# Seven products for eight in two FFN down products of each layer

## The chip, the cores and the metric

The kernel runs on one core of a Trainium2 chip. The metric is the device time of one execution in microseconds (us). A comparison takes the median of several runs. Everything below is float32 in and out.

## The reference, cut to what matters

A two-layer trunk on 256 tokens of width 2048. Each layer has a token mixer (layer 0 a gated linear recurrence, layer 1 a spatial gate) and then a gated FFN of width 5632. The change lies in the last line of the FFN:

```
def conv_ffn(x, w_up, conv_w, conv_b, w_down):
    h = x @ w_up                                  # (256, 2048) @ (2048, 11264)
    a, b = jnp.split(h, 2, axis=-1)
    a = causal depthwise conv of width 3 over a, plus conv_b
    return (jax.nn.silu(a) * b) @ w_down          # (256, 5632) @ (5632, 2048)

h = layer_norm(ALPHA * h + ffn, ln2_g[layer], ln2_b[layer])
```

## The kernel before, in words

**Three products for one.** TensorE multiplies in a 32-bit format that keeps fewer bits than float32. Each float32 operand is therefore cut into a high part (rounded by a cast on ScalarE) and a low part (operand minus high part, on VectorE), and each product is high·high + high·low + low·high. For activations the two parts lie in `X` (input of the up product) and `Y` (input of the down product). Weights are cut as they come.

**Chunks.** A weight chunk is 512 rows by 512 columns: 1 MB, one DMA on SyncE's queue into a `raw` tile of [128, 4, 512]. `convert` makes `whi` (two casts of 128x1024, line 110) and `wlo` (two subtractions of 128x1024, line 111). The tiles `raw`, `whi` and `wlo` have three buffers each, and `AHEAD = 3`: the conversion of chunk n+3 can begin only when TensorE has done with chunk n and gives its buffers back. All chunks of the program stand in one list, `plan`, in the order of use.

**The FFN.** The 5632 inner columns are 11 pieces of 512, in groups `FFN_GROUPS = (3, 4, 4)`. For a group, the *up stage* computes each piece (two blocks of four chunks, `block_b`), with convolution, SiLU and gating on VectorE and ScalarE, and leaves the cut result in `Y`. The *down stage* multiplies `Y` by `w_down`: for each of four blocks of 512 output columns `c`, `block_a` runs over the group's pieces `i`. A chunk there takes 24 matmuls of 128x512: 4 slices of rows, 3 products each, for 2 halves of the tokens `t`. The sum of a block is held in one PSUM bank for each `t`; at the end `add_z` adds it to `z`, the residual sum in SBUF, with one VectorE operation of 128x512 (line 429 in the first group, line 431 after).

**Around it.** The normalisation ahead of the FFN leaves its result in `z` without gain and bias; `residual` (lines 412 and 413) applies them during the first three pieces of the up stage. Then the memory of its eight gain and bias tiles is free, and GpSimd's queue loads the next eight (256 KB each, line 358), which the normalisation after the FFN uses.

**What sets the order.** The kernel is written in one order; a scheduler with buffer pools places the instructions on each engine by priority and readiness when the program is built. On the chip each engine takes its own list in order and waits for what it needs; so does SyncE's DMA queue.

## Time and profile before

| | |
|---|---|
| time, median of 3 runs | 2235.63 us (2235.15 to 2237.25) |
| the profiled execution | 2237.65 us, its span 2235.9 us |
| TensorE matmul busy | 2218.4 us (99%), 12801 matmuls |
| VectorE busy | 1470.1 us (66%) |
| ScalarE busy | 1106.4 us (49%) |
| GpSimd busy | 47.7 us (2%) |
| read from HBM | 425.98 MB, 191 GB/s over the span |

The span is the time from the first to the last instruction in the trace; the rest of the execution's time lies outside of it. "Busy" sums the time in which an engine had an instruction in work. Matmuls overlap in the pipeline, so the mean time of one matmul is not the time that one more or less costs: that is the distance between the starts of two. In a row such as "L431 DVE ... x40 | 27.3, 683 | 33.1 <-PE pa L144 29.2" stand the line of the kernel, the engine, output and inputs, the number of instructions, their sum in us, the mean of one in ns, and the idle time of that engine just before them with what ended it.

### The profile page before, as it was taken

Reading aid. Unit: us, or ns where it says so; the run is one execution under the profiler, and the core shown is the slowest. Engines: PE = TensorE matmul, PEld = TensorE weight load, DVE = VectorE, ACT = ScalarE, POOL = GpSimd, SP = SyncE. Lnnn points to the kernel's source line nnn. Section 1 sums busy time; section 2 is a strip of 40 time slices with the busy share of each in tenths; the row PEclk is TensorE's granted clock in tenths of the full one; section 3 lists DMA queues with packets and bytes.
Section 4 is the critical chain, followed back from the end, with each engine's and each line's share of the span. In section 5 each row is a group of like instructions: output and inputs, shape, how many; then the busy total and the mean of one; then the engine's idle time right before and its main releaser. Section 6 shows DMA issues by size and latency. Waiting matters only on the chain.

```text
span 2235.9 us, 31778 instructions
## 1 busy us (share of the span) xinstructions
PE 2218.4 (99%) x12801; PEld 1913.6 (86%) x12801; DVE 1470.1 (66%) x2309; ACT 1106.4 (49%) x1703; POOL 47.7 (2%) x102
## 2 busy tenths in 40 slices
PE   9999999999999999999999999999999999999998
PEld 8888888889888888888888888888888888888886
DVE  6877677667765666456656686566765666465755
ACT  6656575555444454344445555455544444344542
POOL 3000000000000000000000000000000000000000
PEclk9999999999999999999999999999999999999999
DMA  7454645655565555555555675655565555555553
GB/s 272 156 186 151 202 150 165 215 170 190 198 234 188 192 191 202 189 194 200 190 189 190 205 218 192 229 179 180 188 238 181 203 193 198 192 188 196 182 206 113
DMA packets 214595, 430.13 MB, mean 192 GB/s; under 512 B 7576, under 2 KB 9392, under 8 KB 214448
## 3 DMA queue, kind: packets, MB, share of 16 engines
q1 hardware_dynamic: 210080, 415.26, 55.2%
q0 software_dynamic: 4368, 12.85, 1.9%
q8 instruction: 100, 1.64, 0.3%
q14 instruction: 47, 0.39, 0.0%
HBM read 425.98 MB, written 2.10 MB: 191 GB/s over the span
## 4 chain that ended last, share of the span: by engine, by line
PE 94%; DVE 2%; ACT 2%; issue 1%; DMA 1%; POOL 0%; SPq 0%; DVEq 0%; POOLq 0%; ACTq 0%
PE pb L215 37%; PE pb L222 19%; PE pa L144 12%; PE pa L143 12%; PE pa L142 12%; DVE wlo L111 1%; ACT whi L110 1%; PE pl L652 1%; PE pt L337 1%; PE pg L861 0%; DMA bb<-in_sg_ln_b_dram 0%; DMA z<-in_x_dram 0%; PE pa L784 0%; PE pa L782 0%; PE pa L783 0%
## 5 line engine op out<-in xcount | busy, mean ns | idle before, releaser
L111 DVE TENSOR_TENSOR wlo<-raw,whi 128x1024 fp32r<-128x1024 f32 (+1 forms) x785 | 929.7, 1219 | 656.0 <-ACT whi L110 648.0
L215 PE MATMUL pb<-X,whi 128*128 128x512 f32 (+1 forms) x3960 | 1303.3, 384 | 1.9 <-DVE X L351 1.9
L110 ACT CAST whi<-raw 128x1024 fp32r<-128x1024 f32 (+1 forms) x785 | 790.1, 1048 | 855.2 <-PE pb L215 388.1
L222 PE MATMUL pb<-X,wlo 128*128 128x256 f32 x3840 | 1038.1, 278 | 0.0
L215 PEld LDWEIGHTS pb<-X,whi 128*128 128x128 f32 x3960 | 724.3, 188 | 144.6 <-DVE X L351 2.4
L222 PEld LDWEIGHTS pb<-X,wlo 128*128 128x128 f32 x3840 | 712.5, 188 | 5.9 <-DVE wlo L111 0.3
L143 PE MATMUL pa<-wlo,Y 128*128 128x512 f32 x928 | 361.5, 390 | 0.0
L142 PE MATMUL pa<-whi,Y 128*128 128x512 f32 x928 | 361.5, 390 | 0.0
L144 PE MATMUL pa<-whi,Y 128*128 128x512 f32 x928 | 361.1, 389 | 0.0
L143 PEld LDWEIGHTS pa<-wlo,Y 128*128 128x128 f32 x928 | 174.2, 188 | 36.2
L144 PEld LDWEIGHTS pa<-whi,Y 128*128 128x128 f32 x928 | 174.2, 188 | 35.7
L142 PEld LDWEIGHTS pa<-whi,Y 128*128 128x128 f32 x928 | 174.2, 188 | 35.7
L237 ACT COPY rest<-pb 128x256 f32<-128x256 f32 x240 | 87.5, 369 | 101.6 <-PE pb L215 99.3
L143 PE MATMUL pa<-wlo,X 128*128 128x512 f32 x256 | 99.9, 390 | 0.0
L142 PE MATMUL pa<-whi,X 128*128 128x512 f32 x256 | 99.8, 390 | 0.0
L144 PE MATMUL pa<-whi,X 128*128 128x512 f32 x256 | 99.7, 389 | 0.0
L914 DVE SCALAR_TENSOR_TENSOR act<-a,cols,act 128x254 f32<-128x254 f32 (+1 forms) x176 | 73.0, 475 | 0.0
L144 PEld LDWEIGHTS pa<-whi,X 128*128 128x128 f32 x256 | 48.1, 188 | 9.9
L142 PEld LDWEIGHTS pa<-whi,X 128*128 128x128 f32 x256 | 48.1, 188 | 9.8
L143 PEld LDWEIGHTS pa<-wlo,X 128*128 128x128 f32 x256 | 48.1, 188 | 9.8
L431 DVE TENSOR_TENSOR z<-z,pa 128x512 f32<-128x512 f32 x40 | 27.3, 683 | 33.1 <-PE pa L144 29.2
L918 ACT ACTIVATE act<-act 128x256 f32<-128x256 f32 x88 | 33.8, 415 | 11.7 <-DVE act L914 11.5
(167 smaller groups left out, 1031.8 us busy)
## 6 DMA issues: line engine op xcount, KB each, us to landing
raw<-in_ffn_w_up_dram SPq DMA_DIRECT2D x176, 1024.0 KB, 4.9
raw<-in_ffn_w_down_dram SPq DMA_DIRECT2D x88, 1024.0 KB, 4.9
raw<-in_hg_w_in_dram SPq DMA_DIRECT2D x61, 1024.0 KB, 5.1
raw<-in_sg_w_in_dram SPq DMA_DIRECT2D x32, 1024.0 KB, 5.3
raw<-in_hg_w_out_dram SPq DMA_DIRECT2D x16, 1024.0 KB, 4.9
raw<-in_sg_w_out_dram SPq DMA_DIRECT2D x16, 1024.0 KB, 4.9
g<-in_ln_g_dram POOLq DMA_DIRECT2D x16, 256.0 KB, 5.9
b<-in_ln_b_dram POOLq DMA_DIRECT2D x16, 256.0 KB, 8.9
```

Of the source, the lines that this page charges most:

```text
L110: cast = nc.scalar.copy(hi[:, s, :], raw[:, s, :])
L111: self.last_lo = nc.vector.tensor_tensor(lo[:, s, :], raw[:, s, :], hi[:, s, :].bitcast(F32), ALU.subtract)
L142: nc.tensor.matmul(ps[t], xh, hi[:, kk, :], start=n[t] == 0, stop=False)
L143: nc.tensor.matmul(ps[t], xh, lo[:, kk, :], start=False, stop=False)
L144: nc.tensor.matmul(ps[t], xl, hi[:, kk, :], start=False, stop=last)
L215: return self.nc.tensor.matmul(ps[j][:, :, s], ch[0][:, k % CK, c], act[:, k, :, s], start=start and k == 0, stop=k == last, skip_group_ch ...
L222: return self.nc.tensor.matmul(ps[j][:, 1, :], ch[1][:, k % CK, c], act[:, k, 0, :], start=False, stop=False, skip_group_check=loose,)
L237: nc.scalar.copy(r, ps[:, 1, :])
L337: self.last_turn = nc.tensor.transpose(ps[:, j, :], self.z[:, t, k * P : (k + 1) * P], self.ident)
L431: nc.vector.tensor_tensor(zz, zz, ps, ALU.add)
L914: nc.vector.scalar_tensor_tensor(cv[:, d:], x[:, : S - d], self.c(("cw", l, 2 - d), f), cv[:, d:], ALU.mult, ALU.add,)
L918: nc.scalar.activation(cv, cv, AF.Silu)
```

## The change

In the first two groups of each layer, the product of two pieces (2 x 512 rows) with the column blocks 0 and 1 is taken as a product of 2x2 matrices: the blocks of the left matrix are (token half, piece), those of the right one (piece, column block). The ordinary way takes eight block products of 12 matmuls each; the new one takes seven, and sums of blocks instead:

| product | left block | right block | goes to |
|---|---|---|---|
| 0 | A(0,0) | B(0,0) | z(0,0), and stays in its bank `px` |
| 1 | S0 = A(1,1) - A(1,0) | B(0,0)+B(0,1) | z(1,1), and stays in its bank `py` |
| 2 | S3 | B(1,1) | with 1: z(0,1) |
| 3 | S1 | B(0,0)+B(0,1)+B(1,1) | with 0: z(0,1) |
| 4 | S2 = A(0,0) - A(1,0) | B(0,1)+B(1,1) | with 0, 3: z(1,1) |
| 5 | A(0,1) | B(1,0) | opens the bank of z(0,0), to which ordinary chunks add |
| 6 | A(1,1) | sum of all four | with 0, 3, 4: z(1,0) |

Here A(t,i) is token half t of the i-th piece of the pair. S1 = -S0 - A(0,0) and S3 = -S1 - A(0,1). Signs that the table leaves out are put in when a product is added to or taken from `z`.

- `sums` makes S0 to S3 in float32 from the gated pieces, which are now kept in `act`, and cuts them into `S`: per layer and woven group eight VectorE operations of 128x512 and four casts.
- `make` makes the right blocks: the two raw chunks `b11` and `b12` stay in SBUF in a pool of their own, and the other two, `b2`, pass through `raw`. A block sum is two VectorE additions of 128x1024 (line 161 of the new kernel); there are four. Each of the seven right blocks is converted as a chunk is: seven conversions for four.
- `woven` runs these seven among the ordinary chunks ("N") of the same group, in the order of the table `WOVEN`. The pair is the third and fourth piece of the group of four, and the first two of the group of three (`PAIR`).
- The groups become (4, 3, 4). The last group stays as it was.
- The pool of `b11`, `b12`, `S` and `s` takes the memory in which the next eight gain and bias tiles would lie, and gives it back after the second woven group.

The core of the diff:

```
-FFN_GROUPS = (3, 4, 4)
+FFN_GROUPS = (4, 3, 4)
+PAIR = (2, 0)
+WOVEN = {
+    4: ("N", "N", 0, "N", 1, "N", "N", 2, "N", 3, "N", 4, "N", 5, "N", 6, "N", "N", "N"),
+    3: ("N", 0, "N", 1, "N", 2, "N", 3, "N", "N", 4, 5, 6, "N", "N"),
+}
...
+        def add(out, x, y):
+            for i in range(0, CK, 2):
+                r = slice(i, i + 2)
+                nc.vector.tensor_tensor(out[:, r], x[:, r], y[:, r], ALU.add)
+
+        if which == 0:
+            self.b11 = self.qp.tile([P, CK, NB], F32, tag="b11", name="b11")
+            self.b12 = self.qp.tile([P, CK, NB], F32, tag="b12", name="b12")
+            self.qp.tile([P, PAD2], mybir.dt.uint8, name="pad2")
+            self.load_chunk(self.b11, w, k0, c0)
+            self.load_chunk(self.b12, w, k0, c0 + NB)
+        elif which in (2, 5):
+            self.b2 = self.wp.tile([P, CK, NB], F32, tag="raw", name="raw")
+            self.load_chunk(self.b2, w, k0 + CK, c0 + NB * (which == 2))
+        self.convert(self.b2 if which in (2, 5) else self.b12 if which == 4 else self.b11, False, False)
+        if which == 0:
+            add(self.b11, self.b11, self.b12)
+        elif which == 2:
+            add(self.b11, self.b11, self.b2)
+            add(self.b12, self.b12, self.b2)
+        elif which == 5:
+            add(self.b11, self.b11, self.b2)
...
+        def part(i, f, x, y):
+            s = self.qp.tile([P, CK, P], F32, tag="s", name="s", bufs=2)
+            f(s, x, y)
+            hi = self.S[:, i, :, 0, :]
+            nc.scalar.copy(hi, s)
+            sub(self.S[:, i, :, 1, :], s, hi.bitcast(F32))
+            return s
+
+        s1 = part(0, sub, act1[:, :, t1], act0[:, :, t1])
+        s2 = part(1, neg, s1, act0[:, :, t0])
+        part(3, neg, s2, act1[:, :, t0])
+        part(2, sub, act0[:, :, t0], act0[:, :, t1])
...
+        def product(ps, x, ch, start, stop=True):
+            hi, lo = ch
+            for kk in range(CK):
+                go = dict(skip_group_check=True)
+                nc.tensor.matmul(ps, x(kk, 0), hi[:, kk, :], start=start and kk == 0, stop=False, **go)
+                nc.tensor.matmul(ps, x(kk, 0), lo[:, kk, :], start=False, stop=False, **go)
+                nc.tensor.matmul(
+                    ps, x(kk, 1), hi[:, kk, :], start=False, stop=stop and kk == CK - 1, **go
+                )
...
+        for which in WOVEN[n]:
+            if which == "N":
+                c, i, at, count = left.pop(0)
+                ch = self.chunk(w, (m + i) * CK, c * NB)
...
+            ch = self.taken_seven(which)
...
+            ps = blocks[0] if which == 5 else py if which in (1, 2) else px
+            product(ps, act[which], ch, which in (0, 1, 5), which != 5)
+            if which == 0:
+                gain(0, 0, px)
+            elif which == 1:
+                gain(1, 1, py, True)
+            elif which == 2:
+                gain(0, 1, py, True)
+            elif which == 3:
+                gain(0, 1, px, True)
+            elif which == 4:
+                gain(1, 1, px, True)
+            elif which == 6:
+                gain(1, 0, px)
...
+                    if gi < len(PAIR) and i == PAIR[gi] + 1:
+                        self.sums(*acts[-2:])
+                if gi < len(PAIR):
+                    self.woven(down, m, n, PAIR[gi], m == 0)
...
                 if end:
+                    quads.close()
                     st.close()
                     self.norm("ln2", l, store)
```

`gain` is one VectorE operation of 128x512 on `z`, as in `add_z`.

**VectorE where the first down stage begins (layer 0).** Before, `b` and `Y` are the last operations on the up stage's result, `z` those of `residual`, then come the weight conversions of the down stage:

```order
L244 TENSOR_TENSOR Y<-b,Y 128x256 x2
L238 TENSOR_TENSOR b<-pb,rest 128x256 x2
L923 TENSOR_TENSOR b<-b,act 128x256 x2
L413 TENSOR_TENSOR z<-z,b_4584 128x512
L412 TENSOR_TENSOR z<-z,g_4576 128x512
L244 TENSOR_TENSOR Y<-b,Y 128x256 x2
L413 TENSOR_TENSOR z<-z,b_4584 128x512
L412 TENSOR_TENSOR z<-z,g_4578 128x512 x2
L413 TENSOR_TENSOR z<-z,b_4586 128x512 x2
L111 TENSOR_TENSOR wlo<-raw,whi 128x1024 x6
L429 SCALAR_TENSOR_TENSOR z<-z,pa 128x512 x2
```

Now, from the conversion of product 0's right block on (`b_6909` is `b11`, `b_6910` is `b12`):

```order
L117 TENSOR_TENSOR wlo<-b_6909,whi 128x1024
L406 TENSOR_TENSOR Y<-act,Y 128x256 x2
L189 TENSOR_TENSOR s<-act 128x512
L117 TENSOR_TENSOR wlo<-b_6909,whi 128x1024
L189 TENSOR_TENSOR S<-s,S 128x4x128
L186 SCALAR_TENSOR_TENSOR s<-s,act 128x512
L161 TENSOR_TENSOR b_6909<-b_6909,b_6910 128x1024
L189 TENSOR_TENSOR S<-s,S 128x4x128
L186 SCALAR_TENSOR_TENSOR s<-s,act 128x512
L161 TENSOR_TENSOR b_6909<-b_6909,b_6910 128x1024
L189 TENSOR_TENSOR S<-s,S 128x4x128
L189 TENSOR_TENSOR s<-act 128x512
```

The next row is the conversion of the third ordinary chunk of the stage (`wlo<-raw,whi`, twice). The residual's operations are no longer here, since they end a piece earlier; the sums and the first block sum stand ahead of that conversion instead.

**SyncE's queue in the FFN of layer 0.** Before, the three groups' weights in turn:

```order
L86 DMA raw<-in_ffn_w_up_dram 128x4x512 x24
L86 DMA raw<-in_ffn_w_down_dram 128x4x512 x12
L86 DMA raw<-in_ffn_w_up_dram 128x4x512 x32
L86 DMA raw<-in_ffn_w_down_dram 128x4x512 x16
L86 DMA raw<-in_ffn_w_up_dram 128x4x512 x32
```

Now, from the first up stage to the loads for the second woven group:

```order
L92 DMA raw<-in_ffn_w_up_dram 128x4x512 x29
L150 DMA b_6909<-in_ffn_w_down_dram 128x4x512
L92 DMA raw<-in_ffn_w_up_dram 128x4x512 x3
L150 DMA b_6910<-in_ffn_w_down_dram 128x4x512
L92 DMA raw<-in_ffn_w_down_dram 128x4x512 x5
L150 DMA raw<-in_ffn_w_down_dram 128x4x512
L92 DMA raw<-in_ffn_w_down_dram 128x4x512 x3
L150 DMA raw<-in_ffn_w_down_dram 128x4x512
L92 DMA raw<-in_ffn_w_down_dram 128x4x512
L150 DMA b_8577<-in_ffn_w_down_dram 128x4x512
L92 DMA raw<-in_ffn_w_down_dram 128x4x512 x3
L150 DMA b_8576<-in_ffn_w_down_dram 128x4x512
```

The four loads of each pair are the same in size and number as before; two of them now stand ahead of other weights, go into memory of the new pool, and wait until that is free (`b_8577` and `b_8576` are `b12` and `b11` of the second woven group).

**TensorE at product 1 of the first woven group.** Before, every triple of the down stage reads `Y`:

```order
L142 MATMUL pa<-whi,Y 128x512
L143 MATMUL pa<-wlo,Y 128x512
L144 MATMUL pa<-whi,Y 128x512
L142 MATMUL pa<-whi,Y 128x512
L143 MATMUL pa<-wlo,Y 128x512
```

Now an ordinary chunk ends and product 1, which reads `S`, begins:

```order
L219 MATMUL pa<-whi,Y 128x512
L220 MATMUL pa<-wlo,Y 128x512
L221 MATMUL pa<-whi,Y 128x512
L219 MATMUL pa<-whi,S 128x512
L220 MATMUL pa<-wlo,S 128x512
L221 MATMUL pa<-whi,S 128x512
```

The matmuls are of the same form; a product has 12 of them where an ordinary chunk has 24, and the next ordinary chunk follows it.

## The prediction

> **What bounds the kernel now.** First the page: the engines' shares, the granted clock, the chain that ended last, and the rows of the lines that the change touches.

> ```profile
> PE 2218.4 (99%) x12801; PEld 1913.6 (86%) x12801; DVE 1470.1 (66%) x2309; ACT 1106.4 (49%) x1703; POOL 47.7 (2%) x102
> PEclk9999999999999999999999999999999999999999
> PE 94%; DVE 2%; ACT 2%; issue 1%; DMA 1%; POOL 0%; SPq 0%; DVEq 0%; POOLq 0%; ACTq 0%
> L111 DVE TENSOR_TENSOR wlo<-raw,whi 128x1024 fp32r<-128x1024 f32 (+1 forms) x785 | 929.7, 1219 | 656.0 <-ACT whi L110 648.0
> L143 PE MATMUL pa<-wlo,Y 128*128 128x512 f32 x928 | 361.5, 390 | 0.0
> L144 PE MATMUL pa<-whi,Y 128*128 128x512 f32 x928 | 361.1, 389 | 0.0
> L431 DVE TENSOR_TENSOR z<-z,pa 128x512 f32<-128x512 f32 x40 | 27.3, 683 | 33.1 <-PE pa L144 29.2
> ```

> TensorE is busy for 99% at the full clock, and 94% of the chain is matmuls. The matmuls of `block_a` have 0.0 us of idle time ahead of them in 928 instances. So each matmul taken out of a down stage shortens the kernel by its spacing, as long as TensorE finds its next operands ready. What the spacing is, the timeline of TensorE shows, at the seam between the first up and down stage (start, duration, instruction):

> ```profile
> 634.93 0.39 PE L215 MATMUL pb<-X,whi 128*128 128x512 f32 x1
> 635.15 0.39 PE L142 MATMUL pa<-whi,Y 128*128 128x512 f32 x1
> 635.38 0.39 PE L143 MATMUL pa<-wlo,Y 128*128 128x512 f32 x1
> 635.61 0.39 PE L144 MATMUL pa<-whi,Y 128*128 128x512 f32 x1
> 635.83 0.39 PE L142 MATMUL pa<-whi,Y 128*128 128x512 f32 x1
> ```

> Three matmuls take 635.83 - 635.15 = 0.68 us, so one costs 0.2267 us, though its row lasts 0.39. The seam itself costs nothing. An ordinary chunk of 24 is 5.44 us, a product of 12 is 2.72.

> Next, how much room the other engines have in a down stage: the second one of layer 0, four pieces, by windows, and three moments of VectorE's timeline.

> ```profile
> core 0: us, PE busy (x) PEld busy (x) DVE busy (x) ACT busy (x) POOL busy (x), PEclk, DMA share, GB/s
> 880.00:967.00 87.00, 87.00 (x393) 72.34 (x392) 42.90 (x40) 32.08 (x32) 0.00 (x0) 1.00 0.59 194
> ```

> ```profile
> 633.28 0.75 DVE L238 TENSOR_TENSOR b<-pb,rest 128x256 f32<-128x256 f32 x2
> ...
> 639.70 1.28 DVE L412 TENSOR_TENSOR z<-z,g 128x512 f32<-128x512 f32 x2
> ...
> 642.10 4.62 DVE L111 TENSOR_TENSOR wlo<-raw,whi 128x1024 fp32r<-128x1024 f32 x4
> ```

> TensorE 87.00 of 87.00 us, VectorE 42.90 (49%), ScalarE 32.08 (37%), DMA engines 59% busy at 194 GB/s. VectorE's rows overlap a little: four of 1.219 us end 4.62 us after the first begins, a spacing of (4.62 - 1.219)/3 = 1.134 us; two of 0.68 take 1.28, a spacing of 0.60; two of 0.415 take 0.75, a spacing of 0.335.

> **The change part by part.**

> *Removed.* In each of four places (two groups, two layers) eight block products become seven: 12 matmuls less. 4 x 12 x 0.2267 = 10.88 us off TensorE, which is on the path throughout. Nothing is added to TensorE: the products with `S` have the form of those with `Y`. Groups (4, 3, 4) have the same 11 pieces, and as seams cost nothing, their order does not either.

> *Added on VectorE, per woven group.* Three more conversions, 6 x 1.134 = 6.8 us; four block sums, 8 additions of 128x1024 taken at the row of line 111 (two SBUF inputs, same size), 9.1; 14 gains instead of 8, 6 x 0.683 = 4.1; the sums `S`, 8 x 0.60 = 4.8. Together 24.8 us. In the group of four VectorE then has 38 conversions and 8 additions (46 x 1.134 = 52.2), 14 gains (9.6) and 4.8 of sums: 66.6 us of 12 x 5.44 + 7 x 2.72 = 84.3 (79%). In the group of three, where the sums fall in the up stage of the third piece: 30 + 8 at 1.134 and 14 at 0.683 give 52.7 of 8 x 5.44 + 7 x 2.72 = 62.6 (84%). That is from 49% to 84%, still less than TensorE. It is beside the path, and I cost it at nothing; what hides it is that conversions run up to three chunks ahead.

> *Added on ScalarE.* Three more pairs of casts and four casts of `S`. What it waits for now:

> ```profile
> ACT whi L110 <- PE pa L144: 343.1, 113, 4.9
> 640.79 2.01 ACT L110 CAST whi<-raw 128x1024 fp32r<-128x1024 f32 x2 [2.50 <-PE pa L144]
> 673.43 2.01 ACT L110 CAST whi<-raw 128x1024 fp32r<-128x1024 f32 x2 [3.43 <-PE pa L144]
> ```

> A pair takes 2.01 us and then waits 3.43 for TensorE to give a buffer back: ScalarE is ahead, not short. Fifteen pairs make 30.2 us of 62.6. Cost nothing.

> *The tightest place* is where the first woven group begins, since the sums and the first block sum stand ahead of the third ordinary chunk's conversion. VectorE starts on the last up block at 633.28 in the row above. Behind that stand 12 operations of 128x256 (12 x 0.335 = 4.0 us), two halves of product 0's conversion and two of the block sum (4 x 1.134 = 4.5), seven operations of the sums (7 x 0.60 = 4.2), then the first half of the chunk's conversion (1.22): done at 647.2. TensorE gets there after two ordinary chunks and product 0, 60 matmuls from 635.15: the first matmul that reads `wlo` is due at 635.15 + 61 x 0.2267 = 648.98. Margin 1.7 us, less some semaphores. So no stall here, but this is the term to watch. Before, the same stretch held the residual's last eight operations (4.8 us), which the group of four moves one piece earlier. [...]

> *Moved DMAs.* The weights are the same bytes: 12 chunks of 1.05 MB in 62.6 us are 201 GB/s, against 194 now. `b11` of the first woven group stands in SyncE's queue behind the residual, whose memory it takes, and holds up the `raw` loads behind it; but the residual's operations stand ahead, on VectorE, of the conversion that frees the next `raw` buffer, so it asks for nothing that they don't wait for. In the second woven group `b12` and `b11` wait for the last readers of the first, with a whole up stage to spare.

> The next eight gain and bias tiles can now be loaded only when the woven pool is given back, so this burst of 2 MB moves from the start of the first down stage to the end of the second woven group. What it does there now:

> ```profile
> 642.73 2.12 POOL L358 DMA_DIRECT2D g<-in_ln_g_dram  x4 [217.44 <-DVE z L413]
> 644.84 2.12 POOL L358 DMA_DIRECT2D b<-in_ln_b_dram  x4
> 656.03 2.00 ACT L110 CAST whi<-raw 128x1024 fp32r<-128x1024 f32 x2 [7.79 <-DMA raw<-in_ffn_w_down_dram]
> 658.56 2.00 ACT L110 CAST whi<-raw 128x1024 fp32r<-128x1024 f32 x2 [0.53 <-DMA raw<-in_ffn_w_down_dram]
> DMA to landing us min/median/max: 4.8/4.9/11.7
> ```

> A weight load beside it lands after 11.7 us instead of 4.9, ScalarE waits 7.79 us, and TensorE does not stop, since two chunks lie ready. At the new place two ordinary chunks of 5.44 us follow product 6 and then up chunks of the same length, so the same cover holds. Cost nothing; without cover it is 6.8 us a layer.

> *Sum.* 10.88 us less. The profiled execution took 2237.65 us (span 2235.9), so 2226.8 on that footing; it lies 2.0 us above the median of the three runs, 2235.63. Against the median: **2224.8 us**, 0.49% faster.

> **The rivals.**

> A, *the third chunk is late.* If VectorE waits out ScalarE's cast at each of the four sums (a cast of 128x512 is 0.642 us by the row below) instead of doing other work, 2.6 us are added against a margin of 1.7: 0.9 late in each layer, 2226.6. With a further slip of the same kind at other chunks of the woven groups, up to some 1.5 us in each of the four, 2231. For it: 84% load and products of 2.72 us in a row (4, 5, 6). Against it: other work stands between each sum and its cut.

> ```profile
> L351 ACT CAST X<-turn 128x512 fp32r<-128x512 f32 x24 | 15.4, 642 | 0.0
> ```

> B, *the burst loses its cover.* The moved loads meet a stretch in which three short products have eaten the lead: 6.8 us late in both layers, 13.6, and the time is 2235.63 - 10.9 + 13.6 = 2238.3, no change that counts. It decides only where less than 6.8 us of conversions lie ready; two ordinary chunks are 10.9.

> C, *VectorE becomes the bound: slower.* If each conversion there runs alone, a cast of 1.05 and then two subtractions of 1.219, as the 648.0 us of waits for line 110 might suggest, the group of three needs 15 x 3.49 + 8 x 1.219 + 14 x 0.683 = 71.7 us for 62.6, and the group of four 19 x 3.49 + 9.8 + 9.6 + 4.8 = 90.5 for 84.3. That is 2 x (9.1 + 6.2) = 30.6 us lost for 10.9 won: 2255. Against it: those waits come after VectorE has run out of work, because TensorE holds the buffers (3.43 us in ScalarE's row). A VectorE that is behind finds its casts done, as in the four subtractions of 4.62 us. It decides where VectorE's work in the group of three exceeds 62.6 + 3.8, a quarter above my 52.7: only then does it eat 15 us, which makes the kernel 0.2% slower.

> D, *the removed matmuls do not count.* The path would have to run beside TensorE; the 0.0 idle and the 99% leave no such place. Then 2235.6.

> **How the numbers follow.** 0.2% (4.5 us), about what a measurement of this kernel can tell from no change, puts the bounds at 2231.2 and 2240.1. My forecast, without stalls or with a few tenths: 0.74, 2223.3 to 2226.5 (the three runs spread by 0.5 below and 1.6 above their median). A: 0.14, 2226.5 to 2231. B: 0.05, 2229 to 2238. C: 0.04. D: 0.03. The range must reach well into A: 2222.8 to 2229.5 leaves out a part of A, most of B, and C and D, under 2 in 10. Faster by over 0.2%: the forecast, A and some of B, 0.91. Within: the rest of B, and D, 0.05. Slower: C, 0.04.

> **What would show it.** Right: TensorE has 48 matmuls fewer at the same spacing of 0.2267, no idle ahead of the matmuls of `woven`, including those that read `S`; VectorE near 80% in the woven windows, its conversions now with little or no wait; the GpSimd loads of gain and bias near the end of the second woven group, with a late weight load beside them and no gap on TensorE. Wrong: gaps of TensorE that wait for `wlo` at the third chunk (A), for `whi` after the GpSimd loads (B), or all through the woven groups with VectorE at 95% (C). An addition of 128x1024 well above 1.22 us, or a gain above 0.69, would be the first sign of C.

## The result, and the profile after

| | before | after |
|---|---|---|
| median, runs side by side | 2236.19 us (2235.03 to 2239.29, 6 runs) | 2225.01 us (2224.30 to 2225.96, 6 runs) |
| ratio, 95% interval | | 0.9949 (0.9936 to 0.9962) |
| span of the profiled execution | 2235.9 us | 2223.0 us |

The kernel is 11.2 us faster, 0.5%; 2224.8 us was forecast. First the page of the changed kernel (shares, granted clock, chain), and from the groups with different shapes apart the rows that answer to those before: product matmuls, block sums, gains.

```profile
PE 2205.8 (99%) x12753; PEld 1903.6 (86%) x12753; DVE 1565.5 (70%) x2421; ACT 1139.9 (51%) x1743; POOL 47.9 (2%) x102
PEclk9999999999999999999999999999999999999999
PE 93%; DVE 3%; ACT 2%; issue 1%; DMA 1%; POOL 0%; SPq 0%; DVEq 0%; POOLq 0%; ACTq 0%
L219 PE MATMUL pa<-whi,S 128*128 128x512 f32 x32 | 12.4, 389 | 0.0
L161 DVE TENSOR_TENSOR b<-b,raw 128x1024 f32<-128x1024 f32 x24 | 28.2, 1216 | 0.0
L233 DVE TENSOR_TENSOR z<-z,pa 128x512 f32<-128x512 f32 x28 | 18.7, 681 | 10.6 <-PE pa L221 10.6
```

48 matmuls fewer (12801 to 12753), still 99% busy at the full clock, and the matmuls that read `S` have 0.0 us of idle time ahead of them. VectorE's share rose from 66 to 70%, ScalarE's from 49 to 51%. Next, the two woven down stages of layer 0 by windows: TensorE, weight loads, VectorE, ScalarE, GpSimd, granted clock, DMA share, GB/s.

```profile
678.02:762.34 84.32, 84.32 (x373) 69.82 (x372) 68.20 (x74) 41.37 (x45) 0.00 (x0) 1.00 0.59 200
893.06:955.62 62.56, 62.56 (x277) 51.80 (x276) 51.09 (x60) 31.19 (x36) 4.23 (x8) 1.00 0.55 189
```

From the first matmul of a woven stage to the first of the next, 84.32 and 62.56 us pass, which is 372 and 276 matmuls of 0.2267, with TensorE busy throughout. VectorE is busy for 68.20 and 51.09 us (81 and 82%). The same counts by starts of matmuls give 87.03 and 65.28 us for the ordinary stages of four and three pieces before: 4 x 2.72 = 10.9 us less over two layers. The spans differ by 12.9. The other 2.0 lie outside of these stages, 1.2 of it in how fast the first up piece of each layer ran in the two profiled executions. That pace comes and goes between executions (last section), so I don't count the 2.0 to the change; the timed medians differ by 11.2.

### The profile page after: what moved, and what is told of

Its sections match the earlier page's. It is cut to its first block, busy times and chain, and to the rows that moved or that the text cites. A ratio compares the mean times of both kernels' runs of the same rounds, so it can differ in the third digit from the quotient of the medians.

```text
span 2223.0 us, 31836 instructions
## 1 busy us (share of the span) xinstructions
PE 2205.8 (99%) x12753; PEld 1903.6 (86%) x12753; DVE 1565.5 (70%) x2421; ACT 1139.9 (51%) x1743; POOL 47.9 (2%) x102
## 4 chain that ended last, share of the span: by engine, by line
PE 93%; DVE 3%; ACT 2%; issue 1%; DMA 1%; POOL 0%; SPq 0%; DVEq 0%; POOLq 0%; ACTq 0%
PE pb L377 37%; PE pb L384 19%; PE pa L306 7%; PE pa L305 7%; PE pa L304 7%; PE pa L219 4%; PE pa L220 4%; PE pa L221 4%; DVE wlo L117 1%; PE px L219 1%; PE px L220 1%; PE px L221 1%; ACT whi L116 1%; PE pl L814 1%; PE pt L499 1%
## 5 line engine op out<-in xcount | busy, mean ns | idle before, releaser
L117 DVE TENSOR_TENSOR wlo<-raw,whi 128x1024 fp32r<-128x1024 f32 (+1 forms) x769 | 910.8, 1219 | 545.6 <-ACT whi L116 537.7
L116 ACT CAST whi<-raw 128x1024 fp32r<-128x1024 f32 (+1 forms) x769 | 776.5, 1048 | 752.8 <-PE pb L377 380.7
L305 PE MATMUL pa<-wlo,Y 128*128 128x512 f32 x480 | 187.2, 390 | 0.0
L304 PE MATMUL pa<-whi,Y 128*128 128x512 f32 x480 | 187.1, 390 | 0.0
L306 PE MATMUL pa<-whi,Y 128*128 128x512 f32 x480 | 186.9, 389 | 0.0
L219 PE MATMUL pa<-whi,Y 128*128 128x512 f32 x336 | 130.7, 389 | 0.0
L220 PE MATMUL pa<-wlo,Y 128*128 128x512 f32 x336 | 130.7, 389 | 0.0
L221 PE MATMUL pa<-whi,Y 128*128 128x512 f32 x336 | 130.7, 389 | 0.0
L306 PEld LDWEIGHTS pa<-whi,Y 128*128 128x128 f32 x480 | 90.1, 188 | 18.5
L305 PEld LDWEIGHTS pa<-wlo,Y 128*128 128x128 f32 x480 | 90.1, 188 | 18.5
L304 PEld LDWEIGHTS pa<-whi,Y 128*128 128x128 f32 x480 | 90.1, 188 | 18.5
L221 PEld LDWEIGHTS pa<-whi,Y 128*128 128x128 f32 x336 | 63.1, 188 | 13.1
L220 PEld LDWEIGHTS pa<-wlo,Y 128*128 128x128 f32 x336 | 63.0, 188 | 13.1
L219 PEld LDWEIGHTS pa<-whi,Y 128*128 128x128 f32 x336 | 63.1, 188 | 12.9
```

What stands on the lines that cost most here:

```text
L116: cast = nc.scalar.copy(hi[:, s, :], raw[:, s, :])
L117: self.last_lo = nc.vector.tensor_tensor(lo[:, s, :], raw[:, s, :], hi[:, s, :].bitcast(F32), ALU.subtract)
L219: nc.tensor.matmul(ps, x(kk, 0), hi[:, kk, :], start=start and kk == 0, stop=False, **go)
L220: nc.tensor.matmul(ps, x(kk, 0), lo[:, kk, :], start=False, stop=False, **go)
L221: nc.tensor.matmul(ps, x(kk, 1), hi[:, kk, :], start=False, stop=stop and kk == CK - 1, **go)
L304: nc.tensor.matmul(ps[t], xh, hi[:, kk, :], start=n[t] == 0, stop=False)
```

## The experiments

The kernel before ran beside them. Its median was 2235.4 us beside experiments 1, 2, 3 and 5, 2236.2 beside 4, 7 and the two passes of 6, and 2235.0 beside the one pass of 6. Ratios are against these.

**1. Twelve matmuls put back for each product saved.** Product 5 is repeated into a bank that nothing reads.

```diff
             product(ps, act[which], ch, which in (0, 1, 5), which != 5)
+            if which == 5:
+                product(bank(), act[which], ch, True)
```

> The changed kernel with an eighth block product: product 5 is multiplied a second time into a bank that nobody reads, so that every woven group has 12 matmuls more and all other work of the change stays. My theory: those 48 matmuls at 0.2267 us bring back 10.9 us, and the time is that of before within 1 us, as all added work on VectorE and ScalarE is hidden. Rival (the added work costs something, and the seven products gain more than it): slower than before by that cost. Rival (the matmuls are not the path): like the changed kernel, 11 us faster than before.

Measured: 2236.18 us, ratio 1.0004 (0.9995 to 1.0013). All the added work of VectorE, ScalarE and the moved loads, without the saving, takes the time of before, to within -1.1 to +2.9 us. So what the added work costs is too small to see, and the gain is the 48 matmuls. The repeated product also gives VectorE 2.72 us more in each woven group; that the work stays hidden without it is read from the changed kernel's windows above, where TensorE is busy throughout.

**2. One woven group of the two.**

```diff
-PAIR = (2, 0)
+PAIR = (2,)
```

> Seven products in the first group of each layer alone; the second group has eight. My theory: half the gain, 24 matmuls or 5.4 us faster than before. The gain and bias tiles are then loaded at the end of the first woven group, so up to some tenths may be lost there. Rival (a fixed gain of the order, not of the count): far from half.

Measured: 2230.81 us, ratio 0.9979 (0.9970 to 0.9989), 4.6 us less than before. 24 x 0.2267 = 5.4 lies inside the interval (2.5 to 6.7). By starts of matmuls the first down stage takes 84.32 us as in the changed kernel and the second 65.28 as before, in both layers: each group brings its own half.

**3. The groups alone.** Groups (4, 3, 4) with eight products everywhere.

```diff
-PAIR = (2, 0)
+PAIR = ()
```

> Groups (4, 3, 4) alone, eight products as before. My theory (the number of matmuls sets the time, seams cost nothing): as before, within 1 us, and TensorE's down stages of 384 and 288 matmuls at 0.2267 us. Rival (the gain comes from the new order of the groups or from the residual moved off the seam): 2 to 11 us faster than before.

Measured: 2243.36 us, ratio 1.0040 (1.0028 to 1.0053). A miss: 7.9 us slower than before, though its work is that of before, piece by piece. The rows of GpSimd, ScalarE, VectorE and TensorE in the up stage of the fourth piece (start, duration, then the idle time and what ended it), and TensorE in the other layer:

```profile
642.28 2.12 POOL L520 DMA_DIRECT2D g<-in_ln_g_dram  x4 [217.44 <-DVE z L575]
655.81 1.99 ACT L116 CAST whi<-raw 128x1024 fp32r<-128x1024 f32 x2 [8.00 <-DMA raw<-in_ffn_w_up_dram]
656.89 2.36 DVE L117 TENSOR_TENSOR wlo<-raw,whi 128x1024 fp32r<-128x1024 f32 x2 [7.63 <-ACT whi L116]
659.17 0.75 DVE L400 TENSOR_TENSOR a<-pb,rest 128x256 f32<-128x256 f32 x2
659.64 0.50 PE L377 MATMUL pb<-X,whi 128*128 128x512 f32 x1 [2.29 <-DVE a L400]
...
1664.05 0.50 PE L377 MATMUL pb<-X,whi 128*128 128x512 f32 x1 [3.26 <-DVE a L400]
```

The burst of gain and bias loads still starts when the residual is done, after the third piece; but with a group of four an up stage runs there, not a down stage. ScalarE waits 8.00 us for a late weight load, as it waited 7.79 before. What differs is the queue behind it: VectorE stands at the conversion of the late chunk, and behind that stand the operations (`a<-pb,rest`) that empty the PSUM banks of the up block. TensorE's wait ends with that operation and not with a weight: it runs out of banks, and stops for 2.29 and 3.26 us. The up stages with these stops take 171.75 and 171.54 us. The same work takes 167.98 and 167.97 in the changed kernel and 168.59 and 168.57 in experiment 4, so 6.1 to 7.4 us are lost here, most of the 7.9. The spans differ by only 4.6 (2240.5 against 2235.9), because the profiled execution of before was 2.2 us slower than its median here and this one 1.2 faster.

**4. The groups alone, burst elsewhere.** The burst is held behind a small GpSimd copy that waits for the second group's first column block.

```diff
+        late = nullcontext()
+        if name == "ln2":
+            mark = self.small.tile([P, 6], F32, tag="mark", name="mark")
+            late = self.tc.issue_after(nc.gpsimd.tensor_copy(mark, self.z[:, 1, 0:6]).ins)
+        with late:
+            ...
```

> The kernel e1_groups (groups 4, 3, 4, eight block products) with one edit: GpSimd's queue issues the gain and bias loads of the normalisation after the FFN only behind a small copy that reads z once the second group's first column block has been added, so the 2 MB burst falls into the second down stage instead of the up stage of the fourth piece. My theory (the groups alone cost 7.9 us because the burst delays one weight load of an up stage, behind whose conversion the operations that free TensorE's banks are queued on VectorE): the gap of 2.5 to 3.4 us in each layer goes, and the time is that of the kernel before, 2235.4 us, within 1.5. Rival (the order 4, 3, 4 is itself dearer, by the longer first down stage or by where the residual falls): it stays near 2243.4.

Measured: 2235.15 us, ratio 0.9996 (0.9987 to 1.0005). The 7.9 us are gone, as expected. GpSimd's and ScalarE's rows at the new place, in a down stage:

```profile
913.39 2.13 POOL L520 DMA_DIRECT2D g<-in_ln_g_dram  x4 [0.60 <-ACT whi L116]
917.29 2.01 ACT L116 CAST whi<-raw 128x1024 fp32r<-128x1024 f32 x2 [3.39 <-PE pa L306]
922.73 2.01 ACT L116 CAST whi<-raw 128x1024 fp32r<-128x1024 f32 x2 [3.43 <-PE pa L306]
```

ScalarE's waits beside the burst end with TensorE, none with a DMA. So the order of the groups costs nothing by itself that the interval could show; where the burst falls decides.

**5. The seven products in a row.** The same work as in the changed kernel, in another order.

```diff
-    4: ("N", "N", 0, "N", 1, "N", "N", 2, "N", 3, "N", 4, "N", 5, "N", 6, "N", "N", "N"),
-    3: ("N", 0, "N", 1, "N", 2, "N", 3, "N", "N", 4, 5, 6, "N", "N"),
+    4: ("N", "N", "N", 0, 1, 2, 3, 4, 5, 6) + ("N",) * 9,
+    3: ("N", 0, 1, 2, 3, 4, 5, 6) + ("N",) * 7,
```

> The same seven products in one row behind three (group of four) or one (group of three) ordinary chunks, instead of woven among them. TensorE needs 7 x 2.72 = 19.0 us for the row, VectorE for the conversions, block sums and gains that belong to it 14 x 1.134 + 8 x 1.134 + 6 x 0.683 = 29.0 us, so it falls 10 us behind, of which the lead of up to three chunks covers some 4 to 6. My theory: TensorE stalls 4 to 7 us in each of the four groups, 16 to 28 in all, and the time is 2241 to 2253, slower than before. Rival (the sum over the whole stage decides, and that is still under TensorE's): 2225, as woven.

Measured: 2257.03 us, ratio 1.0095 (1.0080 to 1.0110): 32.0 us more than the changed kernel, and above the 2241 to 2253 expected. The woven stages by windows, and the first stop, on VectorE and TensorE:

```profile
677.98:769.54 91.56, 87.53 (x373) 70.64 (x372) 68.58 (x74) 41.22 (x45) 0.00 (x0) 0.98 0.54 184
900.26:970.92 70.66, 65.56 (x278) 52.38 (x277) 54.08 (x62) 32.00 (x36) 4.24 (x8) 0.98 0.53 180
```

```profile
698.92 2.35 DVE L161 TENSOR_TENSOR b<-b,raw 128x1024 f32<-128x1024 f32 x2
701.19 0.68 DVE L231 SCALAR_TENSOR_TENSOR z<-z,px 128x512 f32<-128x512 f32 x1
701.79 2.35 DVE L117 TENSOR_TENSOR wlo<-b,whi 128x1024 fp32r<-128x1024 f32 x2
...
702.02 0.47 PE L219 MATMUL px<-whi,S 128*128 128x512 f32 x1 [2.12 <-ACT whi L116]
703.06 0.71 PE L220 MATMUL px<-wlo,S 128*128 128x512 f32 x1 [0.57 <-DVE wlo L117]
```

Over the stages VectorE is busy for 68.58 of 91.56 and 54.08 of 70.66 us, less of the time than in the changed kernel, and yet the stages are 7.2 and 8.1 us longer (7.1 and 9.5 in layer 1; 31.9 in all, the whole loss). At 702 us the engine has no idle time between its rows, and TensorE waits first for `whi` of a block sum that VectorE has just made, then for `wlo`. The sum over a stage does not decide; the load of a few chunks in a row does. TensorE's idle time in these stages is 4.0 and 5.1 us (4.0 and 4.9 in layer 1), inside the 4 to 7 expected. The stages lose more than that, in part because the granted clock falls after a stop (0.50 from 703.18 to 706.59 us; last section), which the theory left out.

**6. More VectorE work.** One or two redundant passes behind each half of a block sum.

```diff
                 nc.vector.tensor_tensor(out[:, r], x[:, r], y[:, r], ALU.add)
+                nc.vector.tensor_tensor(out[:, r], out[:, r], out[:, r], ALU.max)
```

> The changed kernel with two redundant passes behind each VectorE block sum (an in-place maximum of the sum with itself, which leaves the values as they are): 16 operations of 128x1024 more in each woven group, 16 x 1.134 = 18.1 us. By sums over a stage VectorE then needs 51.1 + 18.1 = 69.2 of 62.6 us in the group of three and 68.2 + 18.1 = 86.3 of 84.3 in the group of four. Theory 1 (VectorE counts where its sum over the stage exceeds TensorE's): 2 x (6.6 + 2.0) = 17 us more, 2242. Theory 2 (with conversions at most three chunks ahead, it counts wherever some chunks in a row hold more VectorE work than TensorE work, so slack elsewhere in the stage doesn't help): 35 to 45 us more, 2260 to 2270. Theory 3 (VectorE is hidden throughout): 2225.

> The changed kernel with one redundant pass behind each VectorE block sum (an in-place maximum of the sum with itself, values unchanged): 8 operations of 128x1024 more in each woven group, 9.1 us. VectorE's sum is then 51.1 + 9.1 = 60.2 of 62.6 us in the group of three and 77.3 of 84.3 in the group of four, both still below TensorE's. Theory 1 (the sum over a stage decides): no change, 2225.0 within 1.5. Theory 2, now favoured after two passes took 2274.3 (the load of some chunks in a row decides, since conversions are at most three chunks ahead): the three short products behind one another, each with a sum and its pass, no longer fit, and some 6 to 14 us are lost, 2231 to 2239, with gaps of TensorE that wait for wlo.

Measured: two passes 2274.25 us, ratio 1.0166 (1.0152 to 1.0180), 49.2 more than the changed kernel and above the upper end of theory 2, which left out the lower clock too (0.95 and 0.91 over the woven stages of layer 0, 1.00 in the changed kernel); one pass 2237.43, ratio 1.0008 (0.9998 to 1.0017), 12.4 more. With one pass, the woven stages and, in the group of three, VectorE and TensorE:

```profile
677.68:764.28 86.60, 84.92 (x373) 69.66 (x372) 77.01 (x82) 41.36 (x45) 0.00 (x0) 1.00 0.57 195
895.00:961.74 66.74, 64.58 (x278) 52.78 (x276) 60.15 (x68) 31.63 (x36) 4.23 (x8) 0.97 0.53 174
```

```profile
915.90 2.35 DVE L162 TENSOR_TENSOR b<-b 128x1024 f32<-128x1024 f32 x2
918.17 1.22 DVE L161 TENSOR_TENSOR b<-b,raw 128x1024 f32<-128x1024 f32 x1
919.31 0.68 DVE L234 TENSOR_TENSOR z<-z,pa 128x512 f32<-128x512 f32 x1
...
918.11 0.50 PE L220 MATMUL px<-whi,S 128*128 128x512 f32 x1 [0.73 <-ACT whi L116]
920.04 0.80 PE L220 MATMUL pa<-whi,S 128*128 128x512 f32 x1 [1.43 <-DVE z L234]
```

VectorE's 60.15 us are below the 62.56 that TensorE needs, and 77.01 below 84.32, yet the stages grow by 4.2 and 2.3 us. Theory 1 is out. The form of theory 2's stops came out only in part: here the first ends with a cast, and the longer one with a gain (`z<-z,pa`) that frees a bank and stands behind sums and passes in VectorE's queue. In the group of four the stop does end with `wlo`:

```profile
715.85 0.50 PE L221 MATMUL pa<-wlo,Y 128*128 128x512 f32 x1 [1.68 <-DVE wlo L117]
```

**7. A third woven group, without and with the burst held back.** `e7_three` adds the last group of each layer; `e8_late` lets GpSimd issue the burst only behind a copy that waits for the statistics of column block 0.

```diff
-            for c in range(4):
+            left = self.woven_rest(n, END, (2, 1, 0))
+            for which in WOVEN["end"]:
...
+            mark = self.small.tile([P, 6], F32, tag="mark", name="mark")
+            late = self.tc.issue_after(nc.gpsimd.tensor_copy(mark, stats[1][:, 0, :]).ins)
```

> The changed kernel with seven products in the third group of each layer too (pair of its first two pieces, column blocks 2, 1, 0 in one woven stage, block 3 last as before). 24 matmuls less, 24 x 0.2267 = 5.4 us. The pool of the woven tiles is now given back only at the end of the third group's woven stage, so the burst of gain and bias loads falls beside the last four chunks and just ahead of the normalisation. If the removed matmuls are all that counts: 2225.0 - 5.4 = 2219.6. My theory: the burst delays a weight load from 4.9 to about 11.7 us there, and the last chunks have no more than two ready behind three short products; 1.5 to 3 us in each layer come back, 2222 to 2225, and the trace has a gap of TensorE ahead of the last block's chunks.

> e7_three with GpSimd's burst held back until the statistics of column block 0 are taken, so that the last block's four weight loads go ahead of it. My theory: no load is late any more, the last stage still hides the burst, and the whole 5.4 us stay: 2219.6 us (2218.8 to 2220.8). Rival: the held burst lands too late for the normalisation, which then waits for its first gain tile at the seam to the next stage: no better than e7_three, 2222 or more.

Measured: without, 2230.47 us, ratio 0.9972 (0.9961 to 0.9984), 5.5 slower than the changed kernel; held back, 2219.20, ratio 0.9918 (0.9905 to 0.9932), 5.8 faster than it. GpSimd, ScalarE and TensorE without, at the end of layer 1:

```profile
2175.74 2.13 POOL L522 DMA_DIRECT2D g<-in_ln_g_dram  x4 [757.90 <-DVE wlo L119]
2189.05 2.00 ACT L118 CAST whi<-raw 128x1024 fp32r<-128x1024 f32 x2 [7.13 <-DMA raw<-in_ffn_w_down_dram]
2194.02 3.89 ACT L118 CAST whi<-raw 128x1024 fp32r<-128x1024 f32 x4 [2.97 <-DMA raw<-in_ffn_w_down_dram]
...
2197.02 0.51 PE L306 MATMUL pa<-whi,Y 128*128 128x512 f32 x1 [0.82 <-ACT whi L118]
2199.85 0.80 PE L307 MATMUL pa<-wlo,Y 128*128 128x512 f32 x1 [2.33 <-DVE wlo L119]
```

And held back, in layer 0:

```profile
1192.36 3.90 ACT L118 CAST whi<-raw 128x1024 fp32r<-128x1024 f32 x4 [3.20 <-DMA raw<-in_ffn_w_down_dram]
1198.12 2.13 POOL L522 DMA_DIRECT2D g<-in_ln_g_dram  x4
```

Without, two waits for weight loads (7.13 and 2.97 us) come right behind three short products. The lead is used up, TensorE waits for `whi` and `wlo`, and from the first down matmul to the last the stage is 5 us longer in each layer than with the burst held back (83.12 against 78.00, 89.32 against 84.09). I expected 1.5 to 3 and 2222 to 2225, so the size was a miss. Held back, the burst starts behind the last weights' casts, and the saved 24 x 0.2267 = 5.4 us are there. The direction of both came out, and the size of the second (2219.6 forecast).

## Why the prediction was right, and where its reasons were not

- **Removed: right.** 48 matmuls at 0.2267 are 10.88 us; the four stages are shorter by 10.9, and putting the matmuls back brings the time of before back.
- **Added on VectorE and ScalarE, cost 0: right.** 66.6 and 52.7 us of VectorE were worked out, 68.20 and 51.09 stand in the windows; a block sum takes 1.216 us (1.219 was taken), a gain 0.681. Its reason was too simple, as experiments 5 and 6 show: it compared sums over a stage and followed VectorE chunk by chunk at one place only. Rival C's point of decision was put at a quarter more VectorE work than 52.7 us in the group of three; 8 operations more in each woven group (60.15 us in the group of three, 18% above the 51.09) already took the whole gain. The term that was mis-sized is that margin: the cover is three chunks of lead, used up wherever sums and short products stand close. The sevens' places between ordinary chunks are worth 32 us against the same sevens in a row.
- **The tightest place: right.** VectorE's and TensorE's rows at the third ordinary chunk of the first woven group:

```profile
684.54 1.22 DVE L161 TENSOR_TENSOR b<-b,b 128x1024 f32<-128x1024 f32 x1
685.68 0.68 DVE L189 TENSOR_TENSOR S<-s,S 128x512 fp32r<-128x512 f32 x1
686.28 0.68 DVE L186 SCALAR_TENSOR_TENSOR s<-s,act 128x512 f32<-128x512 f32 x1
686.88 1.22 DVE L161 TENSOR_TENSOR b<-b,b 128x1024 f32<-128x1024 f32 x1
...
689.22 2.35 DVE L117 TENSOR_TENSOR wlo<-raw,whi 128x1024 fp32r<-128x1024 f32 x2
691.62 0.39 PE L219 MATMUL pa<-whi,Y 128*128 128x512 f32 x1
691.85 0.39 PE L220 MATMUL pa<-wlo,Y 128*128 128x512 f32 x1
```

  The first half of the conversion ends at 689.22 + 1.22 = 690.44, the matmul that reads it starts at 691.85: 1.4 us of margin, where 1.7 were worked out, and no idle time on TensorE. Rival A fell. Full durations do not add up here either: an operation of 1.22 us is followed by the next after 685.68 - 684.54 = 1.14, one of 0.68 after 0.60, across kinds of operations, so the spacings of 1.134 and 0.60 us that the prediction took hold here too.
- **Moved DMAs: right at the place, wrong for the groups.** The burst went to the end of the second woven group, a weight load came late, and TensorE did not stop:

```profile
940.77 2.12 POOL L520 DMA_DIRECT2D g<-in_ln_g_dram  x4 [515.62 <-DVE wlo L117]
954.40 2.00 ACT L116 CAST whi<-raw 128x1024 fp32r<-128x1024 f32 x2 [7.45 <-DMA raw<-in_ffn_w_up_dram]
```

  But "as seams cost nothing, their order does not either" held only because the pool of the woven tiles pushes the burst out of the way: with that pool left out, the new order alone costs 7.9 us. Rival B's mechanism is real: it showed behind a third woven group, at 5 us a layer where 6.8 were worked out. The late load also stopped TensorE at a place that the prediction had not considered, and by another way, through the banks (experiment 3). The forecast took no harm, because it priced the burst at the place where the pool puts it; but the sentence on the order gave no such reason, and that it held was luck.
- **Conversions with little or no wait: right in the main.** VectorE's waits in the two woven stages of layer 0 (us in total, times, longest) come to 12.4 of 84.3 us and 8.8 of 62.6; over the whole kernel they fell from 648.0 to 550.3.

```profile
DVE wlo L117 <- ACT whi L116: 12.4, 8, 3.1
...
DVE wlo L117 <- ACT whi L116: 8.8, 6, 4.4
...
DVE wlo L117 <- ACT whi L116: 550.3, 250, 5.0
```

## What to carry to other kernels

Price added work on a helper engine against the lead of the buffers (here three chunks), chunk by chunk, not against its share of a stage: at 82% of a stage it was free in one order and cost 32 us in another. When a change moves a pool or a group boundary, look for the transfers that are issued when the memory comes free, and check what stands in the queues behind the one load that they delay. If such a burst lands badly, hold it back on its own queue behind something that marks a safe moment; that alone was worth 11.3 us in `e8_late` against `e7_three`.

## What the runs showed of the hardware

```profile
916.31:919.73 3.42, 1.57 (x6) 0.75 (x4) 3.42 (x4) 2.00 (x2) 0.00 (x0) 1.00 0.00 0
919.73:923.14 3.41, 3.10 (x7) 2.48 (x8) 3.41 (x4) 0.00 (x0) 0.00 (x0) 0.50 0.74 222
...
1916.42:1919.84 3.42, 2.69 (x13) 1.92 (x11) 3.42 (x4) 1.26 (x2) 0.00 (x0) 1.00 0.00 0
1919.84:1923.25 3.41, 1.98 (x8) 1.40 (x9) 3.41 (x4) 0.74 (x1) 0.00 (x0) 1.00 0.28 58
...
1658.90:1662.31 3.41, 1.89 (x11) 1.39 (x9) 1.01 (x1) 2.09 (x3) 0.00 (x0) 1.00 1.03 399
1662.31:1665.73 3.42, 1.68 (x10) 1.51 (x11) 3.42 (x9) 2.10 (x5) 0.00 (x0) 1.00 0.45 129
```

In the row of seven the clock fell to 0.50 for 3.41 us (703.18 to 706.59; the windows give 0.63 from 702.00 to 706.40 and 0.97 from 706.40 to 710.00). With two redundant passes the starts of matmuls go back from 0.43 to 0.23 us apart at 729.23, 944.22, 1749.85 and 1964.85 us: 63, 299 and 362 times 3.413 us behind the first, to within 0.2. A stretch of this length is called a step here, and each window above is one. In layer 0 of the kernel with one pass the two stops fall mostly into one step: TensorE is busy for 1.57 of 3.42 us, and the next step has a clock of 0.50. In layer 1 they are spread over two, with 2.69 and 1.98 us busy, and the clock stays. So in these rows the clock fell after the step with 1.57 us busy, and not after those with 2.69, 1.98, 1.89 and 1.68. This is read from the traces; no run was made to test it, and what sets the fall, and where, was not shown. What the lower clock does is seen with two redundant passes, after a stop of 7.57 us:

```profile
724.00:729.00 5.00, 5.00 (x12) 3.94 (x13) 5.00 (x6) 0.00 (x0) 0.00 (x0) 0.50 0.53 170
729.00:735.00 6.00, 6.00 (x28) 4.94 (x27) 5.66 (x6) 2.80 (x3) 0.00 (x0) 0.99 0.57 209
```

Here 12 matmuls take 5.00 us instead of 2.72. The longest single wait does not tell the cases apart: waits of 2.12 and 0.57 us with one matmul between them (experiment 5) were followed by a clock of 0.50, while in experiment 3 the clock stayed up after a single wait of 3.26 us.

**Still open.** In some profiled executions (before, and several of the experiments) TensorE's spacing in a stretch of the first up piece is 3% wider than in others (132 matmuls from 526 to 549 us before, 136 in the changed kernel), at a granted clock of 1.00, worth 0.6 us a layer. It came and went between kernels that don't differ there, and between the layers of one execution (167.97 and 168.56 us for the first up stages in experiment 5); its cause is not known. Experiment 3 leaves 0.5 to 1.8 of its 7.9 us without a place.
